# Eight of 64 tiles transposed by VectorE instead of TensorE, with another head and another list of transfers

## The chip, the cores and the metric

The kernel runs on one core of a Trainium2 chip. The metric is the device time of one execution in microseconds, the median of three runs. Five engines work in parallel, each through its own list of instructions in order: TensorE (PE in the profile; its weight loads are PEld), VectorE (DVE), ScalarE (ACT), GpSimd (POOL) and SyncE (SP), which here issues every transfer. Sixteen DMA engines move the data.

## The reference

```python
batch, m, k, n = 16, 512, 1024, 768          # all float32
out = np.matmul(x, weight) + bias + residual
```

So 8192 rows of x, each of 1024 numbers, times a matrix of 1024 x 768, plus a bias row and a residual of the size of the output. In all 33.5 MB of x, 25.2 MB of residual and 3.1 MB of weight are read, and 25.2 MB are written.

## The kernel before

**Tiles.** The 8192 rows are cut into four parts (S = 0 to 3) of 16 tiles (j = 0 to 15) of 128 rows; tile t is 16 S + j. Partition p of a part holds the rows 16 p to 16 p + 15, so that a transfer of several tiles reads one long run a partition. SBUF has room for 16 x tiles (`X`) and 32 rows of residual and output (`R`, one 128 x 768 row of tiles each; W is staged there at first too).

**What is done with a tile.** ScalarE casts the x tile to bf16 (`cast`, L226 by way of `copy`) into one of four buffers `XB`. TensorE transposes it (`transp`, L250): two neighbouring bf16 numbers are taken as one 4-byte word, so that four transposes of 128 x 128 words do the 1024 columns. They go to one of two PSUM buffers `PT`, and VectorE copies them to one of four buffers `XT` (L226). Then TensorE does 8 steps (4 q x 2 e) of one weight load (L268) and two matmuls of 512 and 256 columns (L257) into one of three PSUM buffers `PO` (`mm_all`). VectorE's `finish` adds PSUM to an SBUF row (L229). For the first 14 tiles (`EARLY_END`) it adds the bias and puts the sum in a spare row; GpSimd later adds that to the residual row. For the others GpSimd adds the bias to the residual row beforehand (`pool_adds`), and `finish` waits for that. `ADDS` is the order of GpSimd's first 16 adds.

**The order.** `HEAD_ORDER` is a list written by hand for the first three tiles, which go q by q as the parts of W arrive; `warm` are matmuls on zeros. After it a loop runs over t from 3: cast of tile t + 2, GpSimd's adds, the transposes of tile t + 1, all matmuls of tile t, `finish` of tile t - 1. The last tile's columns are done in two parts.

**The transfers.** `ORDER` is the list of all transfers, in the order in which SP issues them: ('x', S, j0, j1) loads x tiles j0 to j1 - 1 of part S, 'r' residual rows, 'w' a quarter of the weight, 'b' the bias; 's' stores rows, 'c' a part of the last row. `pump` takes from its head whatever may be recorded: an x tile needs the cast of the tile 16 before it, a residual row the store of the row 32 before it, a store its `finish` or add. On the chip SP waits at each entry for what it needs, and all that come after it wait too.

**Waits.** `Program.add` records each operation with the keys it reads and writes, and `Program.emit` turns them into waits. [...]

## Time and profile before

| what | value |
|---|---|
| time, median of 3 runs | 210.14 us (210.11 to 210.18) |
| span of the profiled execution | 208.5 us, 2492 instructions |
| PE busy | 201.6 us (97%) |
| DVE busy | 105.3 us (51%) |
| ACT busy | 66.1 us (32%) |
| POOL busy | 115.2 us (55%) |
| transfers | 87.20 MB, 97.9% of 16 engines' span |
| four transposes of a tile, group of 256 | 38.3 us busy |
| copy of transposed words on VectorE, 64 | 44.1 us, 691 ns each |
| last store | issued at 204.63, landed 2.6 us later |

The three runs' times are those of whole executions; the profiled execution is known by its span, and the runs' median lies 1.6 us above that. Busy shares are means over the span; the rows of the profile name an engine, a line of the kernel, an operation, and the tiles it writes and reads. In an order of time, a row has its start, its length, and in brackets how long the engine had been idle and what ended that. Rows of the busy times by stage have, after each engine's time, the granted TensorE clock, the share of the DMA engines and GB/s.

### The profile page before, as it was taken

What the parts mean: (1) busy time and instruction counts of PE and PEld (TensorE: products, weight loads), DVE (VectorE), ACT (ScalarE), POOL (GpSimd) and SP (SyncE); (2) the same over time, 40 slices, a digit from 0 to 9 for tenths busy, and PEclk for the clock granted to TensorE, in tenths of its full rate; (3) what the DMA queues carried; (4) which work ended last, traced back from release to release, by engine and by line L of the source; (5) the groups of instructions that cost most, each with busy time, mean ns of one, the idle gap of its engine ahead of it and who ended that gap; (6) DMA issues with size and microseconds to landing.
All of it is one profiled execution on the core that took longest, in us unless ns stands there. A gap on an engine that the chain in (4) does not pass through costs nothing.

```text
span 208.5 us, 2492 instructions
## 1 busy us (share of the span) xinstructions
PE 201.6 (97%) x1298; PEld 80.8 (39%) x794; DVE 105.3 (51%) x141; ACT 66.1 (32%) x69; POOL 115.2 (55%) x71
## 2 busy tenths in 40 slices
PE   7899999999999999999999999999999999999991
PEld 2333434443443444344334434433443443344340
DVE  1457555445545543654554454555445545544542
ACT  2444522402640282420280094230092047430000
POOL 1100029859999904999029801999207960899200
PEclk9999999999999999999999999999999999999998
DMA  5999999899999999999998999999999999999985
GB/s 216 425 425 445 426 423 475 385 427 425 485 409 416 449 395 438 453 396 437 410 493 387 432 445 429 443 443 385 423 450 468 416 398 471 415 443 417 427 351 232
DMA packets 4627, 87.20 MB, mean 418 GB/s; under 512 B 516, under 2 KB 644, under 8 KB 1416
## 3 DMA queue, kind: packets, MB, share of 16 engines
q1 hardware_dynamic: 4616, 87.05, 97.9%
q8 instruction: 8, 0.13, 0.2%
q14 instruction: 3, 0.02, 0.0%
HBM read 61.88 MB, written 25.17 MB: 417 GB/s over the span
## 4 chain that ended last, share of the span: by engine, by line
PE 92%; DMA 4%; DVE 1%; SPq 0%; ACT 0%; issue 0%
PE psum_o L257 79%; PE pt L250 13%; DMA x_tile<-in_x_dram 4%; SPq L168 0%; DVE xt L226 0%; ACT xb L226 0%; DVE ro L229 0%; SPq L403 0%; SPq L371 0%
## 5 line engine op out<-in xcount | busy, mean ns | idle before, releaser
L257 PE MATMUL psum_o<-w_sb,xt 128*128 128x256 bf16 (+1 forms) x1024 | 176.6, 326 | 0.5 <-DVE xt L226 0.5
L229 POOL TENSOR_TENSOR ro<-ro,bias_sb 128x768 f32<-128x768 f32 x50 | 88.8, 1817 | 46.9 <-DMA ro<-in_residual_dram 46.9
L226 ACT CAST xb<-x_tile 128x1024 bf16<-128x1024 f32 (+1 forms) x63 | 61.3, 1023 | 117.1 <-DMA x_tile<-in_x_dram 88.6
L268 PEld LDWEIGHTS <-xt 128*128 128x128 bf16 x520 | 50.9, 98 | 102.9 <-issue 101.0
L226 DVE COPY xt<-pt 128x1024 bf16<-128x1024 bf16 x64 | 44.1, 691 | 83.4 <-PE pt L250 83.4
L229 DVE TENSOR_TENSOR ro<-psum_o,ro 128x768 f32<-128x768 f32 (+2 forms) x51 | 47.6, 934 | 6.5 <-POOL ro L229 4.5
L250 PE MATMUL pt<-ident,xb 128*128 128x128 f32 x256 | 38.3, 274 | 0.6 <-DVE xb L226 0.4
L229 POOL TENSOR_TENSOR ro<-ro 128x768 f32<-128x768 f32 x14 | 24.9, 1818 | 25.0 <-DMA ro<-in_residual_dram 24.9
L250 PEld LDWEIGHTS pt<-ident,xb 128*128 128x128 f32 x256 | 29.7, 141 | 15.6 <-issue 12.3
L229 DVE TENSOR_TENSOR ro<-psum_o,bias_sb 128x768 f32<-128x768 f32 x14 | 13.2, 948 | 0.0
L312 PE MATMUL psum_o<-warm 128*128 128x512 bf16 x18 | 6.3, 506 | 1.4 <-DVE warm_a L232 1.4
L226 DVE CAST xb<-x_tile 128x512 bf16<-128x512 f32 (+1 forms) x4 | 1.9, 492 | 6.2 <-DMA x_tile<-in_x_dram 6.2
L226 ACT CAST w_sb<-ro 128x768 bf16<-128x768 f32 x4 | 3.3, 832 | 3.7 <-DMA ro<-in_weight_dram 3.7
L226 POOL CAST w_sb<-ro 128x768 bf16<-128x768 f32 x1 | 0.8, 822 | 6.0 <-DMA ro<-in_weight_dram 6.0
L312 PEld LDWEIGHTS psum_o<-warm 128*128 128x128 bf16 x18 | 2.1, 124 | 4.5 <-issue 2.7
L226 DVE CAST w_sb<-ro 128x768 bf16<-128x768 f32 x3 | 1.7, 557 | 2.0 <-DMA ro<-in_weight_dram 2.0
L226 ACT ACT_TABLE_LOAD x1 | 1.3, 1283 | 0.9 <-SPq L371 0.9
L329 DVE STREAM_SHUFFLE bias_sb<-bias_row 128x768 f32<-128x768 f32 x1 | 1.0, 1007 | 0.0
L232 DVE MEMSET warm<- 128x256 uint32 x1 | 0.3, 272 | 1.1 <-SPq L371 1.1
L232 DVE MEMSET bias_row<- 128x768 f32 x1 | 0.7, 698 | 0.2 <-issue 0.2
L232 POOL MEMSET ident<- 128x128 f32 x1 | 0.2, 204 | 0.5 <-SPq L371 0.5
L320 POOL TENSOR_SCALAR_AFFINE_SELECT ident<-ident 128x128 f32<-128x128 f32 x1 | 0.3, 292 | 0.2 <-POOL ident L232 0.2
(7 smaller groups left out, 0.7 us busy)
## 6 DMA issues: line engine op xcount, KB each, us to landing
out_dram<-ro SPq DMA_DIRECT2D x3, 6144.0 KB, 34.6
x_tile<-in_x_dram SPq DMA_DIRECT2D x3, 5120.0 KB, 24.5
ro<-in_residual_dram SPq DMA_DIRECT2D x3, 3840.0 KB, 32.4
x_tile<-in_x_dram SPq DMA_DIRECT2D x3, 3072.0 KB, 34.0
ro<-in_residual_dram SPq DMA_DIRECT2D x3, 2304.0 KB, 18.7
x_tile<-in_x_dram SPq DMA_DIRECT2D x4, 1024.0 KB, 10.9
x_tile<-in_x_dram SPq DMA_DIRECT2D x2, 2048.0 KB, 23.4
out_dram<-ro SPq DMA_DIRECT2D x1, 3840.0 KB, 13.3
```

Source lines behind the costliest of these rows:

```text
L226: op(eng, lambda e: (e.copy if eng == "act" else e.tensor_copy)(out=dst, in_=src), rd, wr)
L229: op(eng, lambda e: e.tensor_add(out=dst, in0=a, in1=b), rd, wr)
L232: op(eng, lambda e: e.memset(dst, v), [], [wr])
L250: op("pe", lambda e, q=q: e.transpose(out=pt[:, q, :], in_=words[:, ts(q, P)], identity=ident), [("XB", t % XB_N, 2 * q // n_q), "ident"], ...
L257: return e.add_instruction(mybir.InstMatmult(name=nc.get_next_instruction_name(), ins=[e.lower_ap(rhs), e.lower_ap(lhsT, for_matmul_weight ...
L268: op("pe", lambda g: g.ldweights(lhsT), rd)
L312: op("pe", lambda e: e.matmul(PO[i][:, 0:512], lhsT=warm[:, 0:P], rhs=warm, start=True, stop=True), ["warm"], [("PO", i)])
L320: op("pool", lambda e: e.affine_select(out=ident, in_=ident, compare_op=mybir.AluOpType.not_equal, fill=1.0, base=0, pattern=[[-1, P]], ch ...
L329: op("dve", lambda e: e.stream_shuffle(out=bias_sb, in_=bias_row, mask=[0] * QUAD), ["bias_row"], ["bias"])
```

## The change

Four pairs of tiles, (21, 22), (45, 46), (52, 53) and (60, 61), are no longer transposed on TensorE. Each pair is cast by ScalarE into a buffer of its own (`XB2`), six tiles before its first tile instead of two. VectorE then transposes it (`blocks`) from SBUF to SBUF (`XT2`): the 128 x 128 words of a block are cut into 4 x 4 squares of 32 x 32, and one instruction takes the squares (a, b) of all four q and both tiles from partitions 32 a to 32 a + 31, transposes each, and writes them to partitions 32 b to 32 b + 31. That is 16 instructions of 32 partitions x 256 words a pair, in place of two copies of 128 x 1024 bf16. `turn` places two of them behind `finish` and two behind the next copy, in each of the four turns of the loop from d - 5 to d - 2, where d is the pair's first tile.

In every turn of the loop the transposes of tile t + 1 now stand between the two halves of the matmuls of tile t, and `finish` of tile t - 1 before them on VectorE.

In the head, tile 3 is loaded behind W, cast and transposed at the end, and three warming matmuls go. GpSimd's first 16 adds are in the order of the tiles. The list of transfers has other cuts: x tiles 10 to 15 of part 0 in one, behind eight residual rows instead of six; the x parts cut at 9, 7 and 8 instead of 6; the store of part 1 cut at 11.

```diff
+DT = [21, 45, 52, 60]
+DT_LEAD = 6
-ADDS = [10, 14, 3, 2, 4, 15, 11, 1, 5, 13, 7, 6, 12, 9, 0, 8]
+ADDS = [0, 1, 2, 3, 4, 5, 6, 7, 8, 9, 10, 11, 12, 13, 14, 15]
 HEAD_ORDER = [('cast', 0, 'v'), ('cast', 1, 's'), ('tr', 0), ('tr', 1), ('wc', 0, 0, 's'), ('wc', 0, 1, 'g'),
- ('warm', 3), ('mm', 0, 0), ('mm', 1, 0), ('cast', 2, 'sv'), ('cast', 3, 'sv'), ('warm', 3),
- ('tr', 2), ('tr', 3), ('wc', 1, 0, 's'), ('wc', 1, 1, 'v'), ('mm', 2, 0), ('mm', 0, 1),
- ('mm', 1, 1), ('mm', 2, 1), ('wc', 2, 0, 's'), ('wc', 2, 1, 'v'), ('mm', 0, 2), ('mm', 1, 2),
- ('mm', 2, 2), ('wc', 3, 0, 's'), ('wc', 3, 1, 'v'), ('bias',), ('cast', 4, 'sv'), ('mm', 0, 3),
- ('fin', 0), ('mm', 1, 3), ('mm', 2, 3)]
-ORDER = [('x', 0, 0, 2), ('w', 0, 0, 2), ('x', 0, 2, 4), ('w', 1, 0, 2), ('b', 0, 0, 0), ('w', 2, 0, 2),
- ('w', 3, 0, 2), ('x', 0, 4, 6), ('x', 0, 6, 10), ('r', 0, 0, 6), ('x', 0, 10, 14),
- ('r', 0, 6, 16), ('x', 0, 14, 16), ('x', 1, 0, 6), ('r', 1, 0, 6), ('x', 1, 6, 16),
- ('r', 1, 6, 16), ('s', 0, 0, 16), ('x', 2, 0, 6), ('r', 2, 0, 6), ('x', 2, 6, 16),
- ('r', 2, 6, 16), ('s', 1, 0, 16), ('x', 3, 0, 6), ('r', 3, 0, 7), ('x', 3, 6, 16),
- ('r', 3, 7, 16), ('s', 2, 0, 16), ('s', 3, 0, 10), ('s', 3, 10, 13),
- ('s', 3, 13, 15), ('c', 3, 15, 0), ('c', 3, 15, 1)]
+ ('warm', 3), ('mm', 0, 0), ('mm', 1, 0), ('cast', 2, 'sv'), ('tr', 2), ('mm', 2, 0), ('wc', 1, 0, 's'),
+ ('wc', 1, 1, 'v'), ('mm', 0, 1), ('mm', 1, 1), ('mm', 2, 1), ('bias',), ('wc', 2, 0, 's'),
+ ('wc', 2, 1, 'v'), ('mm', 0, 2), ('mm', 1, 2), ('mm', 2, 2), ('wc', 3, 0, 's'), ('wc', 3, 1, 'v'),
+ ('cast', 3, 'sv'), ('mm', 0, 3), ('fin', 0), ('mm', 1, 3), ('tr', 3), ('mm', 2, 3), ('cast', 4, 's')]
+ORDER = [('x', 0, 0, 2), ('w', 0, 0, 2), ('x', 0, 2, 3), ('w', 1, 0, 2), ('b', 0, 0, 0), ('w', 2, 0, 2),
+ ('w', 3, 0, 2), ('x', 0, 3, 4), ('x', 0, 4, 6), ('x', 0, 6, 10), ('r', 0, 0, 8), ('x', 0, 10, 16),
+ ('r', 0, 8, 16), ('x', 1, 0, 9), ('r', 1, 0, 6), ('x', 1, 9, 16), ('r', 1, 6, 16), ('s', 0, 0, 16),
+ ('x', 2, 0, 7), ('r', 2, 0, 8), ('x', 2, 7, 16), ('r', 2, 8, 16), ('s', 1, 0, 11), ('x', 3, 0, 8),
+ ('r', 3, 0, 8), ('s', 1, 11, 16), ('x', 3, 8, 16), ('r', 3, 8, 16), ('s', 2, 0, 16), ('s', 3, 0, 10),
+ ('s', 3, 10, 13), ('s', 3, 13, 15), ('c', 3, 15, 0), ('c', 3, 15, 1)]
...
     def transp(t):
-        if t < n_t:
+        if t < n_t and t not in two:
...
+    two = {t + i: i for t in DT for i in range(2)}
+
+    def blocks(t, n0, n1):
+
+        src = XB2.bitcast(FP32).rearrange("p i (q c) -> p i q c", c=P)
+        dst = XT2.rearrange("p i q m e -> p i q (m e)").bitcast(FP32)
+        for n in range(n0, n1):
+            a, b = divmod(n, P // QUAD)
+            op("dve", lambda e, a=a, b=b: e.transpose(
+                out=dst[ts(b, QUAD), :, :, ts(a, QUAD)], in_=src[ts(a, QUAD), :, :, ts(b, QUAD)]),
+               [("XB2", 0), ("XB2", 1)], [("XT2", n)])
...
+    per = (P // QUAD) ** 2
+
+    def turn(h):
+        for d in DT:
+            i, n = h - 2 * (d - DT_LEAD + 1), 2 * (DT_LEAD - 2)
+            if 0 <= i < n:
+                blocks(d, per * i // n, per * (i + 1) // n)
+
     for t in range(HEAD, n_t):
-        cast(t + 2)
+        for d in DT:
+            if t == d - DT_LEAD:
+                cast(d)
+                cast(d + 1)
+        if t + 2 not in two:
+            cast(t + 2)
         pool_adds(t + 1)
-        transp(t + 1)
         if t < n_t - 1:
-            mm_all(t, range(n_q))
+            mm_all(t, range(n_q // 2))
         finish(t - 1)
         pool_adds(t + 1)
+        turn(2 * t)
+        transp(t + 1)
+        turn(2 * t + 1)
+        if t < n_t - 1:
+            mm_all(t, range(n_q // 2, n_q))
```

More of the change, by code (lines that the diff above doesn't have):

```diff
@@ L151 @@
     XT = fixed(sb, "xt", XT_N, [P, n_q, P, 2], BF16)
+    (XB2,) = fixed(sb, "xb_two", 1, [P, 2, K], BF16)
+    (XT2,) = fixed(sb, "xt_two", 1, [P, 2, n_q, P, 2], BF16)
     PO = fixed(ps, "psum_o", HEAD, [P, N], FP32)
@@ L238, in cast @@
             rd, wr = [("X", t % XR)], [("XB", t % XB_N, i) for i in range(2)]
+            if t in two:
+                dst, wr = XB2[:, two[t], :], [("XB2", two[t])]
             if how == "sv":
@@ L267, in mm @@
         lhsT, rd = XT[t % XT_N][:, q, :, e], [("XT", t % XT_N)]
+        if t in two:
+            lhsT, rd = XT2[:, two[t], q, :, e], [("XT2", n) for n in range((P // QUAD) ** 2)]
         op("pe", lambda g: g.ldweights(lhsT), rd)
```

## The prediction

> **What bounds the kernel now.** I read the page from the top: busy shares, slices, transfer queues, the chain that ended last.

> ```profile
> PE 201.6 (97%) x1298; PEld 80.8 (39%) x794; DVE 105.3 (51%) x141; ACT 66.1 (32%) x69; POOL 115.2 (55%) x71
> ...
> DMA  5999999899999999999998999999999999999985
> ...
> q1 hardware_dynamic: 4616, 87.05, 97.9%
> ...
> PE 92%; DMA 4%; DVE 1%; SPq 0%; ACT 0%; issue 0%
> ```

> Two resources are full at once. TensorE (PE) is busy 97% and carries 92% of the chain. But the transfer engines are busy 97.9% of the same span, and a faster TensorE takes no byte away. So I asked next where the transfer engines have any room, with the busy times by stage:

> ```profile
> 3.00:190.00 187.00, 185.85 (x1206) 74.41 (x731) 96.17 (x128) 64.66 (x67) 110.37 (x63) 1.00 1.01 431
> 190.00:200.00 10.00, 10.00 (x68) 3.88 (x39) 5.56 (x8) 0.00 (x0) 4.09 (x3) 1.00 0.96 412
> 200.00:204.00 4.00, 4.00 (x26) 1.93 (x20) 2.18 (x3) 0.00 (x0) 0.00 (x0) 1.00 0.77 325
> 204.00:206.00 2.00, 0.14 (x2) 0.00 (x0) 0.42 (x1) 0.00 (x0) 0.00 (x0) 1.00 0.98 391
> ```

> The last but one number is the DMA share: 1.01 from 3 to 190 us, 0.96 for ten microseconds, 0.77 for four. The mean engine waits for results for 0.4 + 0.9 us in the tail. The slowest engine does not wait at all. The landing records of the last five stores end at 201.69, 204.44, 206.28, 206.93 and 207.27 us. These steps of 2.75, 1.84, 0.65 and 0.34 us are what eight packets of 347, 232, 84 and 45 ns take. The next slowest engine lands the last store 0.3 us earlier, the fastest 0.5. So there are two ends side by side: compute earlier by any amount brings almost nothing, and compute later by more than about 0.4 us (between 0.3 and 0.5) shows in full.

> The steady state of one tile, in order of time:

> ```profile
> 25.25 0.60 PE L250 MATMUL pt<-ident,xb 128*128 128x128 f32 x4
> ...
> 25.68 2.76 PE L257 MATMUL psum_o<-w_sb,xt 128*128 128x512 bf16 x16
> 25.89 0.69 DVE L226 COPY xt<-pt 128x1024 bf16<-128x1024 bf16 x1 [1.48 <-PE pt L250]
> ...
> 26.50 0.95 DVE L229 TENSOR_TENSOR ro<-psum_o,bias_sb 128x768 f32<-128x768 f32 x1
> ...
> 28.29 0.60 PE L250 MATMUL pt<-ident,xb 128*128 128x128 f32 x4
> ```

> A tile takes 28.29 - 25.25 = 3.035 us (as exact over many tiles); its matmuls take 28.29 - 25.68 = 2.60, its four transposes the other 0.435. VectorE (DVE) does one copy and one add, 1.64 us, and then waits 1.48 us.

> **The change part by part.** The profiled span is 208.5 us and the median of the runs 210.14, so 1.6 us lie around the span; I add differences to the median.

> *Removed from TensorE:* 4 transposes of 8 tiles, 8 x 0.435 = 3.48 us, all on PE's path.

> *Added to VectorE:* 16 strips a pair, 64 in all, each 32 partitions x 256 words; 8 copies of 0.691 go. The trace has no strip. Its nearest rows:

> ```profile
> L229 DVE TENSOR_TENSOR ro<-psum_o,ro 128x768 f32<-128x768 f32 x49 | 46.5, 949 | 5.6 <-POOL ro L229 4.5 <-PE psum_o L257 1.1
> ...
> L329 DVE STREAM_SHUFFLE bias_sb<-bias_row 128x768 f32<-128x768 f32 x1 | 1.0, 1007 | 0.0
> ...
> L232 DVE MEMSET warm<- 128x256 uint32 x1 | 0.3, 272 | 1.1 <-SPq L371 1.1
> ...
> L229 DVE TENSOR_TENSOR ro<-psum_o,ro 128x256 f32<-128x256 f32 x1 | 0.4, 425 | 0.2 <-PE psum_o L257 0.2
> ```

> The low bound is the memset of 256 words, 272 ns. The add of 256 words takes 425. The two adds give (949 - 425)/512 = 1.02 ns an element; the shuffle, the nearest in kind, less 512 elements is 1007 - 524 = 483 ns, the high bound. I take 440 ns, just above the add of the same size. On average that is harmless: 64 x 0.44 - 8 x 0.69 = 22.6 us more, 128 of 208 us busy. But the strips are not spread: `turn` puts four into each of four tile periods before a pair, between the add and the copy that the next tile's matmuls wait for. In such a period VectorE has 0.949 + 0.691 + 4 x 0.44 = 3.40 us to do, and TensorE 3.035.

> Does it overlap? Two full-width adds in a row take 1.82 us (at 18.61), 0.08 less than twice 0.949. With 0.08 off at six hand-overs the load is 2.92 us, under 3.035. No pair in the trace goes from one group of partitions to another, as each strip does; I give no credit for an overlap that only full-width pairs show, and keep 2.92 as the other end. [...]

> At 3.40 VectorE slips 0.365 a period. In the first period of a window the copy ends about 0.15 + 0.95 + 0.88 + 0.69 = 2.67 us after the matmuls' start, 0.3 before it is needed (0.06 for the hand-over). So the next copies are late by 0.07, 0.365 and 0.365: 0.8 us of PE wait a pair, 3.2 for four, against 0.87 saved a pair.

> *The head.* x tile 3 (0.52 MB, 1.2 us at the rate below) now lies behind W, so W's last three parts land 1.2 us earlier and tile 3 starts at about 18.4 instead of 19.6. One round of three warming matmuls goes too; it stood in a wait. This gain is spent at once, by

> *the list of transfers.* Tiles 10 to 13 came by themselves; now 10 to 15 come in one, behind eight residual rows instead of six. ScalarE and GpSimd show when transfers landed:

> ```profile
> 34.93 3.89 ACT L226 CAST xb<-x_tile 128x1024 bf16<-128x1024 f32 x4 [7.81 <-DMA x_tile<-in_x_dram]
> 46.47 1.99 ACT L226 CAST xb<-x_tile 128x1024 bf16<-128x1024 f32 x2 [7.66 <-DMA x_tile<-in_x_dram]
> ```

> Between them 10 residual rows and 2 x tiles, 4.98 MB, took 11.54 us: 0.432 MB/us. Two rows and two tiles more are 1.84 MB, 4.25 us, so tile 10 lands at 39.2 and its cast (1.04) ends at 40.2. Its transposes stand in the middle of tile 9, due at 18.4 + 6 x 3.035 + 1.3 = 37.9. TensorE waits 2.4 us, and tile 10 starts at 40.3 + 0.435 + 1.3 = 42.05, where it stood at 22.65 + 6 x 3.035 = 40.86: 1.2 us later, head included. The later x parts land before their casts by 2 us or more, but for tile 16, where I find ScalarE level with TensorE: the casts of 21 and 22 (1.94 us) now precede that of 17. SP's queue stays fed: the one new wait on it, that of the last residual part for the split-off store of part 1 to land, begins with 8 x tiles (4.19 MB, 9.7 us) still queued.

> *The order of the adds.* GpSimd gets residual rows at 31.85 (30.03 before, two rows more), does 8 at 1.78, waits for 46.5, does six, and finishes add 14 at 58.9, 15 at 60.7. VectorE's add of tile 14 is ready at 57.2 and waits 1.7 us there; the copy of 16 behind it ends at 60.5 where 60.2 was due: 0.3. Row 16 lands at 62.9 (46.47 plus 7.08 MB at the rate above), so GpSimd's add of it ends at 64.7; VectorE, behind add 15, one add, four strips and a copy, is there at 64.2. That costs the first window another 0.5.

> *The transposes in the middle of a tile* cost nothing outside the windows: the copy ends 2.7 us after the tile's start, due at 3.04. That cover of 0.3 is what the strips use up.

> Sum on TensorE: 1.2 + 0.3 + 0.5 + 3.2 - 3.48 = 1.7 us later at the end. Less the 0.4 that the slowest transfer engine hides: 1.3 us, **211.4**.

> **The rivals.**

> *Strips overlap, or cost under 0.41 us in a row (load up to 3.30).* Then TensorE ends up to 2 us earlier (1.2 + 0.3 - 3.48) and the slowest transfer engine sets the end as now. Nothing shrinks its work: the same bytes, one transfer more (eight packets an engine; under 0.1 us by the fixed time that 309 ns for a packet of 8 KB and 611 for one of 16 KB leave). 210.1, between 209.8 and 210.5. For it: DMA share 1.01. Against it: the add of 256 words already takes 0.425.

> *A gap at every hand-over.* The cast that ends at 6.45 releases TensorE at 6.50: a waited-for hand-over takes 0.05. With 0.06 at six hand-overs the load is 3.76, 0.725 a period, 2.1 us a pair: 1.2 + 0.3 + 0.5 + 8.4 - 3.48 = 6.9 later on TensorE, 216.6. At the high bound of 483 ns without gaps the load is 3.57 and a pair costs 1.4: 4.1 later, 213.8; at 425 ns it is 3.34 and 0.58, and the time 210.6.

> *The tail shrinks.* If the engines' spread (2.3 us at the tenth row of the last store) comes out smaller, earlier results let go of the 1.3 us that the mean engine waits: up to 209.1. It decides only if VectorE keeps up and the slowest engine loses its lag of 1.3 us; I see nothing that makes it.

> **How the numbers follow.** About 0.2%, 0.42 us, can be told from no change. Strips without overlap at 425 to 483 ns, 210.6 to 213.8: 0.38. Overlap, end set by transfers: 0.40, of which 0.32 within 0.2%, 0.04 on either side. Gaps as well, 213.8 to 218: 0.15. The tail shrinks: 0.07, all faster. Faster 0.11, same 0.33 (0.01 of it from the first case's edge), slower 0.56. The range from 209.8 to 216.3 leaves out most of the shrunken tail and the upper part of the gaps; the forecast case's own range is 210.6 to 213.8.

> **What would show it.** Right: strips of about 440 ns starting no earlier than the one before ends; TensorE's weight loads waiting for VectorE's copies, 0.3 to 0.4 us at three tiles before each pair, and some 2 us for the cast of tile 10; VectorE busy near 128 us; transfer share over the span a little lower. Wrong: strips in a row at under 0.41 us, no such waits, TensorE done by 203 and the last store landing at 207 as before. The forecast also falls if the wait at tile 10 is absent, or if a transfer starves.

## The result, and the profile after

The changed kernel takes 213.34 us (median of 4 runs, 213.27 to 214.57), the kernel before 210.12 (4 runs, 209.97 to 210.18). The ratio is 1.0164, interval 1.0145 to 1.0184: slower by 3.2 us, where the forecast was slower by 1.3. The span of the profiled execution went from 208.5 to 211.5 us. Two of the kernels below (the spread strips and fewer bytes) each had one execution of over 740 us; without it their medians would be lower by at most 0.07 us.

The page of the kernel after, the lines that answer to those of before:

```profile
PE 198.5 (94%) x1239; PEld 77.1 (36%) x759; DVE 132.4 (63%) x196; ACT 66.8 (32%) x69; POOL 115.3 (55%) x71
...
q1 hardware_dynamic: 4760, 87.05, 96.5%
...
PE 44%; DMA 22%; DVE 21%; POOL 6%; issue 3%; SPq 2%; DVEq 0%; POOLq 0%
...
L267 DVE STREAM_TRANSPOSE xt_two<-xb_two 32x256 f32<-32x256 f32 x64 | 27.9, 435 | 1.1
```

TensorE is busy 3.1 us less, close to the 3.48 that were saved on it, and ends later: it waits more. The chain of work that ended last shows on whom. It was 92% TensorE; now half of it goes through residual transfers, VectorE and GpSimd. A strip takes 435 ns.

The busy times by stage of the kernel after. The columns are the stretch, its length, then PE, PEld, DVE, ACT and POOL, the granted clock, the share of the transfer engines and GB/s. The share counts each transfer packet whole in the stretch in which it starts, so in short stretches it can be above 1, or 0 while older packets still run:

```profile
3.00:190.00 187.00, 179.76 (x1131) 69.73 (x687) 119.91 (x177) 64.33 (x66) 112.39 (x64) 1.00 1.01 430
190.00:200.00 10.00, 9.59 (x59) 3.25 (x34) 7.09 (x11) 1.05 (x1) 2.17 (x2) 1.00 0.84 359
200.00:204.00 4.00, 4.00 (x29) 1.73 (x18) 1.98 (x3) 0.00 (x0) 0.00 (x0) 1.00 0.87 367
204.00:206.00 2.00, 2.00 (x12) 0.88 (x9) 1.31 (x2) 0.00 (x0) 0.00 (x0) 1.00 0.29 110
```

Up to 190 us the transfer engines are as full as before. Then their share falls to 0.84 (0.96 before), and between 204 and 206 us they have almost nothing to do (0.29) while TensorE is fully busy; before, TensorE was done by then. Compute now sets the end alone. TensorE ends at 207.52 (204.14 before, +3.38), the last store lands at 210.23 (207.27 before, +2.96). The 0.42 between the two differences is the part that the slowest transfer engine used to hide.

VectorE in the second half of one window, the kernel after, in order of time:

```profile
141.43 0.96 DVE L231 TENSOR_TENSOR ro<-psum_o,ro 128x768 f32<-128x768 f32 x1
142.41 0.88 DVE L267 STREAM_TRANSPOSE xt_two<-xb_two 32x256 f32<-32x256 f32 x2
143.30 0.69 DVE L228 COPY xt<-pt 128x1024 bf16<-128x1024 bf16 x1
144.02 0.89 DVE L267 STREAM_TRANSPOSE xt_two<-xb_two 32x256 f32<-32x256 f32 x2
144.92 0.96 DVE L231 TENSOR_TENSOR ro<-psum_o,ro 128x768 f32<-128x768 f32 x1
```

No row has a bracket: VectorE waits for nobody, and one round takes 144.92 - 141.43 = 3.49 us, where TensorE's tile takes 3.035. TensorE waits for the rest. The waits of its weight loads in the kernel after (total us, times, longest):

```profile
PEld L286 <- DVE xt L228: 12.0, 20, 1.0
```

### The profile page after: what moved, and what is told of

Its sections match the earlier page's. It is cut to its first block, busy times and chain, and to the rows that moved or that the text cites. A ratio compares the mean times of both kernels' runs of the same rounds, so it can differ in the third digit from the quotient of the medians.

```text
span 211.5 us, 2498 instructions
## 1 busy us (share of the span) xinstructions
PE 198.5 (94%) x1239; PEld 77.1 (36%) x759; DVE 132.4 (63%) x196; ACT 66.8 (32%) x69; POOL 115.3 (55%) x71
## 3 DMA queue, kind: packets, MB, share of 16 engines
q1 hardware_dynamic: 4760, 87.05, 96.5%
## 4 chain that ended last, share of the span: by engine, by line
PE 44%; DMA 22%; DVE 21%; POOL 6%; issue 3%; SPq 2%; DVEq 0%; POOLq 0%
PE psum_o L273 39%; DMA ro<-in_residual_dram 22%; DVE xt_two L267 9%; DVE ro L231 7%; POOL ro L231 6%; DVE xt L228 5%; PE pt L254 5%; SPq L170 2%; SPq L438 0%; DVEq L104 0%; POOLq L104 0%; SPq L406 0%
## 5 line engine op out<-in xcount | busy, mean ns | idle before, releaser
L273 PE MATMUL psum_o<-w_sb,xt 128*128 128x256 bf16 (+1 forms) x875 | 154.4, 325 | 5.1 <-DVE xt L228 3.6
L228 ACT CAST xb<-x_tile 128x1024 bf16<-128x1024 f32 (+1 forms) x55 | 54.7, 1028 | 113.1 <-PE pt L254 67.5
L286 PEld LDWEIGHTS <-xt 128*128 128x128 bf16 x456 | 44.6, 98 | 96.6 <-issue 81.5
L228 DVE COPY xt<-pt 128x1024 bf16<-128x1024 bf16 x56 | 38.6, 691 | 30.8 <-PE pt L254 30.5
L254 PE MATMUL pt<-ident,xb 128*128 128x128 f32 x224 | 33.6, 273 | 2.3 <-ACT xb L228 2.3
L254 PEld LDWEIGHTS pt<-ident,xb 128*128 128x128 f32 x224 | 26.0, 140 | 15.7 <-issue 11.3
L267 DVE STREAM_TRANSPOSE xt_two<-xb_two 32x256 f32<-32x256 f32 x64 | 27.9, 435 | 1.1
L273 PE MATMUL psum_o<-w_sb,xt_two 128*128 128x256 bf16 (+1 forms) x125 | 21.9, 325 | 0.2
L286 PEld LDWEIGHTS <-xt_two 128*128 128x128 bf16 x64 | 6.3, 98 | 13.6 <-issue 13.6
L228 ACT CAST xb_two<-x_tile 128x1024 bf16<-128x1024 f32 x8 | 8.0, 1043 | 7.9 <-DMA x_tile<-in_x_dram 7.9
```

The costliest lines, as they stand in the source:

```text
L228: op(eng, lambda e: (e.copy if eng == "act" else e.tensor_copy)(out=dst, in_=src), rd, wr)
L254: op("pe", lambda e, q=q: e.transpose(out=pt[:, q, :], in_=words[:, ts(q, P)], identity=ident), [("XB", t % XB_N, 2 * q // n_q), "ident"], ...
L267: op("dve", lambda e, a=a, b=b: e.transpose(out=dst[ts(b, QUAD), :, :, ts(a, QUAD)], in_=src[ts(a, QUAD), :, :, ts(b, QUAD)]), [("XB2", 0) ...
L273: return e.add_instruction(mybir.InstMatmult(name=nc.get_next_instruction_name(), ins=[e.lower_ap(rhs), e.lower_ap(lhsT, for_matmul_weight ...
L286: op("pe", lambda g: g.ldweights(lhsT), rd)
```

## The experiments

All edits are to the kernel after.

**No pairs.** Everything else of the change stays.

```diff
-DT = [21, 45, 52, 60]
+DT = []
```

> The changed kernel with no pair on VectorE (DT empty): all 64 tiles transposed by TensorE, the new head, list, order of adds and place of the transposes kept. Theory (two causes: overloaded windows on VectorE, and a late start of tiles 10 to 16): in the changed kernel's trace the four windows stretch 12 tile periods by 5.1 us over 3.04 each, 0.36 of which the two short tiles behind them give back, so 4.7 us go, and 3.48 us of transposes come back: 213.3 - 1.3 = 212.1 us. Rival A (the strips are the whole loss): about 210.1 us, as before. Rival B (the head, the list and the adds are the whole loss, the windows hide behind it): 213.3 us.

Measured: 212.06 us (6 runs, two of them 2 us longer than the others), ratio to the kernel before 1.0079 [1.0062, 1.0096]. The pairs with their strips cost 213.34 - 212.06 = 1.28 us net, although they take 3.48 us off TensorE. The other 1.9 us belong to the rest of the change.

**The strips spread.** The same 16 strips a pair over six tile periods instead of four, at most three in one; two pairs moved by one tile, so that a window, which now begins a tile earlier, does not begin before the tiles of the pair ahead of it are multiplied. It ran twice.

```diff
-DT = [21, 45, 52, 60]
+DT = [21, 45, 53, 61]
...
-    per = (P // QUAD) ** 2
+    SLOTS = [0, 1, 1, 2, 1, 2, 1, 2, 1, 2, 3, 0]
...
-            i, n = h - 2 * (d - DT_LEAD + 1), 2 * (DT_LEAD - 2)
-            if 0 <= i < n:
-                blocks(d, per * i // n, per * (i + 1) // n)
+            i = h - 2 * (d - DT_LEAD)
+            if 0 <= i < len(SLOTS):
+                blocks(d, sum(SLOTS[:i]), sum(SLOTS[:i + 1]))
```

> The changed kernel with the strips of a pair spread thinner: 1 at the end of the loop's turn d - 6, 3 in each of d - 5 to d - 2, 3 in d - 1, where no copy is made; so that a period holds 0.957 + 0.70 + 3 x 0.445 = 2.99 us on VectorE instead of 3.49 against 3.04 on TensorE. Pairs at 21, 45, 53, 61, so that a pair's strips do not start before the one before it is used. Theory (load over the period makes the wait): no wait of 0.45 us at three tiles before each pair, at most 0.3 at the pair's first tile; TensorE done 3 to 4 us earlier than 207.5, and the time at the transfer engines' end, 210.1 to 210.4 us. Rival A (strips cost by their number, wherever they stand): 213.3. Rival B (the late start is the loss): 212.5 to 213.3 us.

> The changed kernel with strips spread 1, 3, 3, 3, 3, 3 and pairs 21, 45, 53, 61, once more, for its profile: 210.9 us as measured before. Theory: no waits of 0.45 us before the pairs 45, 53 and 61; the waits at tiles 10 and 16 as in the changed kernel; TensorE done near 204 us and the last store landed at 207.3 to 208.

Measured: 210.94 us the first time, ratio 1.0041 [1.0023, 1.0059], and 211.02 the second, 1.0048 [1.0028, 1.0067]. Spreading alone takes back 2.3 to 2.4 of the 3.2 us. The pairs that cost 1.28 now gain 212.06 - 210.98 = 1.1. The ten runs of the second time lie in two groups, five at 210.3 to 210.6 and five at 211.5 to 211.9; the second group has a lower mean granted clock (0.987 to 0.990 against 0.995 to 1.000). What may lie behind that is in the last section. In the first group, to which the profiled execution belongs, spreading takes back 2.9 of the 3.2 us: TensorE ends at 204.50 instead of 207.52, no tile before the pairs 45, 53 and 61 starts late any more, and the waits at tiles 10 (2.2 us) and 16 are about as in the kernel after.

**The old list of transfers and the old order of GpSimd's adds, in part 0 and 1.** The first pair goes, because its window would need x tiles that this list brings later. The pairs' windows are those of the change.

```diff
-DT = [21, 45, 52, 60]
+DT = [45, 52, 60]
...
-ADDS = [0, 1, 2, 3, 4, 5, 6, 7, 8, 9, 10, 11, 12, 13, 14, 15]
+ADDS = [10, 14, 3, 2, 4, 15, 11, 1, 5, 13, 7, 6, 12, 9, 0, 8]
...
- ('w', 3, 0, 2), ('x', 0, 3, 4), ('x', 0, 4, 6), ('x', 0, 6, 10), ('r', 0, 0, 8), ('x', 0, 10, 16),
- ('r', 0, 8, 16), ('x', 1, 0, 9), ('r', 1, 0, 6), ('x', 1, 9, 16), ('r', 1, 6, 16), ('s', 0, 0, 16),
+ ('w', 3, 0, 2), ('x', 0, 3, 4), ('x', 0, 4, 6), ('x', 0, 6, 10), ('r', 0, 0, 6), ('x', 0, 10, 14),
+ ('r', 0, 6, 16), ('x', 0, 14, 16), ('x', 1, 0, 6), ('r', 1, 0, 6), ('x', 1, 6, 16), ('r', 1, 6, 16), ('s', 0, 0, 16),
```

> The changed kernel with the old list of transfers for parts 0 and 1 from x tile 6 on and the old order of adds; the pair (21, 22), which that list can't serve in time, is left to TensorE; the other three pairs and their four strips a period stay. Theory: the wait of 2.3 us at tile 10 and that of 0.4 us at tile 16 go, with them the first window (1.68 us of waits, 0.87 saved): 213.3 - 3.5 = 209.8, so the transfer engines' end, 210.1 us; up to 211.4 us if the add of row 16, done at 63.8 us in the kernel before, now holds back the copy of tile 18 that stands behind it on VectorE. Rival A (strips are the whole loss): three quarters of 3.2 us stay, 212.5 us. Rival B (list and head are the loss): 210.1 us.

Measured: 212.07 us, ratio 1.0087 [1.0071, 1.0102]: a miss by 2 us. VectorE of this kernel, in order of time, shows why:

```profile
63.77 0.96 DVE L231 TENSOR_TENSOR ro<-psum_o,ro 128x768 f32<-128x768 f32 x1 [2.98 <-POOL ro L231]
64.64 0.68 DVE L228 COPY xt<-pt 128x1024 bf16<-128x1024 bf16 x1
```

The add waits 2.98 us for GpSimd, and the copy, whose input is long ready, waits behind it. TensorE's next matmuls then wait 0.98 us for that copy. The same place in the kernel before:

```profile
62.33 0.69 DVE L226 COPY xt<-pt 128x1024 bf16<-128x1024 bf16 x1 [1.48 <-PE pt L250]
63.80 0.96 DVE L229 TENSOR_TENSOR ro<-psum_o,ro 128x768 f32<-128x768 f32 x1 [0.78 <-POOL ro L229]
65.36 0.69 DVE L226 COPY xt<-pt 128x1024 bf16<-128x1024 bf16 x1 [0.61 <-PE pt L250]
```

The add waits here too, and ends at 64.76, but the copy stood ahead of it. The next copy still finds VectorE idle for 0.61 us, so nothing reaches TensorE. This is a part of the change that the forecast had not priced: `finish` now stands ahead of the copy.

**Both repairs.** The old list and order of adds with the spread strips, on the pairs 45, 53 and 61; `ORDER`, `ADDS` and `SLOTS` as in the two diffs above.

```diff
-DT = [21, 45, 52, 60]
+DT = [45, 53, 61]
```

> Both: the old list of parts 0 and 1 and the old order of adds, pairs 45, 53, 61, strips spread 1, 3, 3, 3, 3, 3. TensorE should be done by 203.5 us, earlier than the 204.1 of the kernel before. Theory (the slowest transfer engine sets the end): 210.1 us, within 0.3, whatever TensorE saves. Rival C (TensorE sets the end): below 209.5 us. Rival D (strips or the new place of the transposes cost something not yet seen): above 210.6 us.

Measured: 210.48 us, ratio 1.0014 [1.0004, 1.0024], with TensorE done at 203.97. VectorE of this kernel in a spread window:

```profile
136.57 0.96 DVE L231 TENSOR_TENSOR ro<-psum_o,ro 128x768 f32<-128x768 f32 x1
137.55 0.43 DVE L267 STREAM_TRANSPOSE xt_two<-xb_two 32x256 f32<-32x256 f32 x1
137.99 0.69 DVE L228 COPY xt<-pt 128x1024 bf16<-128x1024 bf16 x1
138.71 0.88 DVE L267 STREAM_TRANSPOSE xt_two<-xb_two 32x256 f32<-32x256 f32 x2
139.61 0.96 DVE L231 TENSOR_TENSOR ro<-psum_o,ro 128x768 f32<-128x768 f32 x1
```

With three strips the round is 139.61 - 136.57 = 3.04 us, TensorE's own period: VectorE is full and, in the spread windows, holds nobody up. The fourth strip is what the windows of the change do not fit.

**No pairs, with the old list and the old order of adds.** `ORDER` and `ADDS` as in the diff of the old list.

```diff
-DT = [21, 45, 52, 60]
+DT = []
```

> No pair on VectorE, the old list of transfers for parts 0 and 1 and the old order of adds; what stays of the change is the new head and the new place of finish and the transposes in a tile's period. Theory (finish, which waits for GpSimd's add of a row that has just landed, now stands ahead of the copy that TensorE waits for): in the run with the old list TensorE lost 1.2, 0.7 and 0.6 us at tiles 18, 24 and 34 this way, 2.5 in all; less 0.5 us gained in the head and 0.4 hidden by the transfer engines: 210.1 + 1.6 = 211.7 us. Rival (what is left of the change costs nothing): 210.1 us.

Measured: 211.40 us, ratio 1.0064 [1.0049, 1.0079]. Against 212.06 without pairs, list and order of adds are worth 0.66.

**The copy ahead of `finish` again**, in the kernel above.

```diff
-        finish(t - 1)
-        pool_adds(t + 1)
         turn(2 * t)
         transp(t + 1)
+        finish(t - 1)
+        pool_adds(t + 1)
         turn(2 * t + 1)
```

> The kernel before this one in the list with a single swap: the transposes and their copy are recorded ahead of finish of tile t - 1, still in the middle of the period. Theory: the waits at tiles 18, 24 and 34 go, TensorE ends some 0.5 us before the 204.1 of the unchanged kernel, and the transfer engines set the end: 210.1 us. Rival (the middle of the period is itself the loss, since the copy has 1.3 us less room): 211.7 us as without the swap.

Measured: 210.41 us, ratio 1.0020 [1.0010, 1.0030]. Moving two lines is worth 0.99 us. VectorE of this kernel, where the wait for GpSimd is as long as in the kernel before and again falls behind the copy:

```profile
62.98 0.69 DVE L228 COPY xt<-pt 128x1024 bf16<-128x1024 bf16 x1 [1.48 <-PE pt L254]
64.43 0.96 DVE L231 TENSOR_TENSOR ro<-psum_o,ro 128x768 f32<-128x768 f32 x1 [0.77 <-POOL ro L231]
```

**The copy first, and nothing else**: the diff just shown, in the kernel after, with its windows, list and order of adds.

> The changed kernel with that swap alone: pairs, list and adds as changed. Theory: the wait of 0.45 us at tile 16 and the 0.5 us that the first window loses to GpSimd's adds go; the wait at tile 10 (2.3) and the overload in the windows (0.455 a period) stay: 213.3 - 0.9 = 212.4 us, and at least 212. Rival A (strips are the whole loss): 213.3. Rival E (the order on VectorE is the whole loss): 210.1 us.

Measured: 214.77 us, ratio 1.0227 [1.0212, 1.0242], slower by 1.4 than the kernel after: a miss. TensorE does end some 0.6 us earlier. But in a full window the strips and the copy now come before the add, and the add that the store of the last ten tiles waits for starts at 192.84 instead of 190.84. The store is issued at 193.82 (191.83 after), and the busy times by stage of this kernel show that the transfer engines began nothing until then:

```profile
191.00:194.00 3.00, 2.71 (x18) 0.79 (x9) 2.90 (x6) 1.05 (x1) 1.78 (x2) 1.00 0.00 0
```

A DMA share of 0.00 says that no packet starts in these three microseconds. By the start and length of every packet, the mean transfer engine stands idle for 3.6 us between 189 and 195, against 1.7 in the kernel after. So the transfers have work to the very end again, and what TensorE gained is lost: fifteen of the sixteen engines land the last store by 210.08, where the kernel after is done at 210.23. The sixteenth engine lands it at 211.80, 1.7 us behind the others, which is more than the whole slowdown. An instruction fetch of 16 KB, 0.96 us long, starts at 204.52 among the last stores and can be a part of that lag; the trace does not say on which engine it ran, and the rest stays open. In these kernels, then, the copy first gains where VectorE has room (0.99 us without pairs) and nothing in full windows.

**All repairs.** The kernel of both repairs with the copy first as well.

```diff
-        finish(t - 1)
-        pool_adds(t + 1)
         turn(2 * t)
         transp(t + 1)
+        finish(t - 1)
+        pool_adds(t + 1)
         turn(2 * t + 1)
```

> Old list and old adds, pairs 45, 53 and 61 with strips spread 1, 3, 3, 3, 3, 3, and the copy ahead of finish. TensorE should be done near 201.5 to 202 us, 2 to 2.5 us before the unchanged kernel. Theory (the slowest transfer engine sets the end): 210.1 us, within 0.2, last store landed at 207.0 to 207.3 as before. Rival C (TensorE sets the end): 208 us or less.

Measured: 210.50 us, ratio 1.0023 [1.0010, 1.0036]. TensorE's last result is stored from 202.52, against 204.63 in the kernel before, 2.1 us earlier, and the last store lands at 207.41, against 207.27. Compute was made faster, as the change set out to do, and nothing came of it. The time is even 0.4 us above the 210.1 that the theory named, as it is with both repairs; that rest is open. The stages of this kernel:

```profile
200.00:204.00 4.00, 2.03 (x14) 1.09 (x12) 1.70 (x3) 0.00 (x0) 0.00 (x0) 1.00 0.93 387
204.00:206.00 2.00, 0.00 (x0) 0.00 (x0) 0.00 (x0) 0.00 (x0) 0.00 (x0) 0.93 0.82 329
```

TensorE is idle from 202 us, while the transfer engines work at 0.93 and 0.82.

**Fewer bytes.** The kernel above without loading the last four residual rows of part 3 (1.57 MB, 3.6 us at the measured 0.432 MB/us); these four tiles are added to what lies in SBUF. It ran twice.

```diff
+                nl = nj - 4 if (S, j0) == (3, 8) else nj
-                dma(R[:, t0 % RR:t0 % RR + nj, :], res_d[S, :, j0:j1, :], [], rows(t0, t0 + nj))
+                dma(R[:, t0 % RR:t0 % RR + nl, :], res_d[S, :, j0:j0 + nl, :], [], rows(t0, t0 + nl))
```

> The kernel with everything mended (old list and adds, spread strips, copy first; 210.5 us, TensorE done at 202), with the last four residual rows left unloaded: their adds take what lies in those rows. 1.57 MB less, 3.6 us of the transfer engines; all engines' work stays. Theory (the transfer engines' bytes set the end of that kernel): 3.6 us less on the slowest engine, until the end is set by the last add, 202.5 plus 2.3 us to land: 207.5 to 208.2 us. Rival (the last results set the end): 210.5 us, no change.

> The kernel with fewer bytes once more, for where its time goes: it came out at 209.14 us where 207.5 to 208.2 was expected. If the transfer engines still set the end, TensorE is done near 202.0 and the last store lands 2 us or more after the last result is handed over, with the engines' share near 1.0 to the end. If TensorE sets it, TensorE is done near 204 and the last store lands within about 3 us of it. The time should be 209.1 again.

Measured: 209.14 us, ratio 0.9956 [0.9939, 0.9972], then 209.33, ratio 0.9962 [0.9943, 0.9982]. Fewer bytes and the same compute are faster by 1.2 to 1.4, so the transfers do set the end there; TensorE is done at 202.0 in both kernels. Only a third of the 3.6 us came, and the repeat shows where most of the rest is:

```profile
186.00:188.30 2.30, 2.30 (x17) 0.93 (x10) 2.21 (x5) 1.05 (x1) 2.30 (x2) 1.00 0.35 150
```

The transfer engines finish their earlier work one after the other, from 186.98 to 189.72 us, and the store of the last ten tiles is issued at 188.27, the moment VectorE's add of the tenth ends (188.24). By the start and length of every packet, the mean engine stands idle for 1.35 us between 186 and 189.6. With all bytes no engine stands idle in this stretch (its share is 1.09 from 186 to 188.3). About 1 us is left, and the landing records say where it lies, not why: fourteen engines land the last store by 204.90, one at 205.32 and the last at 206.24. So neither picture of the repeat's expectation holds in full: TensorE is done at 202.0, but the share is only 0.27 from 204 to 206 us.

**Do strips overlap at all?** Each strip of the kernel after cut into two halves of 32 x 128 words, which lie on the same partitions one after the other. One run.

```diff
-            op("dve", lambda e, a=a, b=b: e.transpose(
-                out=dst[ts(b, QUAD), :, :, ts(a, QUAD)], in_=src[ts(a, QUAD), :, :, ts(b, QUAD)]),
-               [("XB2", 0), ("XB2", 1)], [("XT2", n)])
+            for i in range(2):
+                op("dve", lambda e, a=a, b=b, i=i: e.transpose(
+                    out=dst[ts(b, QUAD), i, :, ts(a, QUAD)], in_=src[ts(a, QUAD), i, :, ts(b, QUAD)]),
+                   [("XB2", 0), ("XB2", 1)], [("XT2", n)])
```

> The changed kernel with each strip cut into two of 128 words, one for each tile of the pair: two in a row now read and write the same partitions, while every second hand-over still changes them. It measures the hand-over by itself; the time will be longer, 217 to 221 us, as a period holds eight halves. From the strip of 435 ns for 256 words and 1.02 ns a word, a half takes about 305 ns. Theory (a hand-over between different partitions gives no overlap): within a pair of halves the second starts about 80 ns before the first ends, as two full-width adds do; from pair to pair it starts 0 to 20 ns after the end. Rival (a transposing instruction never overlaps): no overlap within a pair either.

Measured: 224.37 us, slower than expected. The group of halves of this kernel, and VectorE in order of time:

```profile
66.31 1.28 DVE L268 STREAM_TRANSPOSE xt_two<-xb_two 32x128 f32<-32x128 f32 x4
67.61 0.69 DVE L228 COPY xt<-pt 128x1024 bf16<-128x1024 bf16 x1
...
L268 DVE STREAM_TRANSPOSE xt_two<-xb_two 32x128 f32<-32x128 f32 x128 | 38.7, 302 | 3.3
```

A half takes 302 ns, where half a strip would be 218: 435 = 302 + 128 x 1.04 ns, so some 170 ns of each strip would not depend on its size, an estimate from these two sizes. Four halves take 1.28 us, not the 1.21 of four times 302: the second half starts 34 ns after the first has ended, the next pair, on other partitions, 13 ns after. No strip overlaps the one before it, on the same partitions or not. So the rival holds here, not the theory. Behind an add it is otherwise. In the kernel after:

```profile
60.98 0.96 DVE L231 TENSOR_TENSOR ro<-psum_o,ro 128x768 f32<-128x768 f32 x1 [0.29 <-POOL ro L231]
61.86 0.87 DVE L267 STREAM_TRANSPOSE xt_two<-xb_two 32x256 f32<-32x256 f32 x2
```

The first of these strips starts at the same partitions as the add and 84 ns before the add has ended; a strip on other partitions starts 14 ns after an add (at 142.41, for one).

## Why the prediction was right or wrong

The direction and the mechanism were right; the size was not. Set against the forecast's sum, with the starts of tiles (their first weight load) in the two traces (us on TensorE):

| step of the sum | forecast | measured |
|---|---|---|
| tile 10 late, head included | +1.2 | +1.70 |
| copy of 16 behind `finish` | +0.3 | +0.40 |
| row 16, in the first window | +0.5 | +0.55 |
| four windows | +3.2 | +4.21 |
| transposes saved | -3.48 | -3.48 |
| TensorE's end | +1.7 | +3.38 |
| hidden by the slowest transfer engine | -0.4 | -0.42 |

**The strip and what stands about it.** 440 ns were forecast and 435 measured, without overlap between strips. x tiles 10 to 15 were to land at 39.2 and their first cast starts at 39.24; TensorE was to wait 2.4 us and waits 2.30; residual row 16 was to land at 62.9 and GpSimd's add of it starts at 63.04:

```profile
39.24 5.87 ACT L228 CAST xb<-x_tile 128x1024 bf16<-128x1024 f32 x6 [11.99 <-DMA x_tile<-in_x_dram]
40.34 0.66 PE L254 MATMUL pt<-ident,xb 128*128 128x128 f32 x4 [2.30 <-ACT xb L228]
59.14 0.96 DVE L231 TENSOR_TENSOR ro<-psum_o,ro 128x768 f32<-128x768 f32 x1 [2.23 <-POOL ro L231]
67.50 1.47 PE L273 MATMUL psum_o<-w_sb,xt 128*128 128x512 bf16 x8 [0.51 <-DVE xt L228]
```

These are lines of the order of time of the kernel after: arrival, wait, and the two places where GpSimd's order reaches TensorE by way of VectorE's copy.

**The step that failed first: the windows.** The load of a round was put at 3.40 us, without gaps, and was 3.49. Its instructions take 3.39 of it (the strips a little less than forecast, the add 0.957 instead of 0.949); the other 0.10 are gaps at the six hand-overs to or from a strip: 31 ns after the copy, about 14 at the others. The slip is 0.455 a round, not 0.365. And the forecast counted 0.07 in the first full round and two more slips, where the second, third and fourth windows lose 0.22 to 0.25, then 0.45, then 0.46 to 0.48 in their rounds, 1.14 to 1.16 each in all. The first loses 0.55 more, to row 16. Together 5.14, of which 0.38 come back in the two short tiles behind each window: 4.76 with row 16, against 3.7. The gaps were a rival's term (0.06 at six hand-overs, 216.6). It was kept apart from the likeliest case as if a gap were all or nothing; the small one that was there lay between the two.

**The second: tile 10.** The new start of tile 10 was forecast at 42.05 and is 42.03, and the old one, forecast at 40.86, is 40.76. Both were right within 0.1 and their difference was not the lag. In the kernel before, a tile's start comes after the transposes of the next tile; in the changed one these come in the middle. At the end of the tile the changed kernel is 42.03 + 3.035 - 40.76 - 2.60 = 1.70 late. The two starts of tile 3, 19.39 and 18.34, compare in the same false way: the head gained 1.05 - 0.435, about 0.6, where the forecast took 1.2.

**The third: "the transposes in the middle of a tile cost nothing outside the windows".** The cover of 0.3 us holds only while `finish` does not wait. Ahead of the copy, `finish` hands GpSimd's lateness to TensorE. With the new list and adds this was in the sum in part (0.3 and 0.5); with the old list it cost 0.99 us by itself, which the forecast had no term for. It is no part of the miss in the table, whose terms close; it is a wrong step that another list would have made dear.

**The rivals.** Strips that overlap fall with 435 ns, the rounds of 3.49 us and the halves. The engines' spread did come out smaller, 0.2 us at the tenth row of the last store (202.18 to 202.38) where it was 2.3, but only because all of them had waited for VectorE's add; with TensorE as the end, that gained nothing. The 1.3 us of waiting that this rival built on were too many: read from the shares by stage they are 0.4 + 0.9, by the start and length of every packet 0 + 0.56. VectorE is busy 132.4 us where about 128 were named, and its copies hold up TensorE by 0.45 us in a full round where 0.3 to 0.4 were.

**The end.** The 0.4 us that the transfers hide were right. The two fulls that the forecast put side by side were shown: with all repairs TensorE is done 2.1 us earlier and the time stays at 210.5.

Going back from after to before by medians: spread strips give back 2.3 to 2.4. By another path, without the pairs 1.28, with the old list and adds 0.66, with the copy first 0.99, which leaves 210.41 against 210.07. These steps are not independent: the copy first brings 0.99 there, and with the full windows that kernel is slower by 1.4. The last 0.3 us is partly the landing (207.39 against 207.27); the rest is open, as are 0.2 of the 3.2 us that lie around the span (1.84 us after, 1.6 before). No kernel here that does the whole work beats the one before.

## What to carry to other kernels

When work moves from a full engine to one with idle time, add up the receiving engine's work in the stretch where it lands, gaps included, and compare that with the other's period; a mean share of 63% hid rounds of 3.49 us against 3.04. Put the instruction that the full engine waits for ahead of one that itself may wait for a third engine, as long as the engine that runs both has room. And before speeding up one engine, ask what ends next to it: here the slowest transfer engine had work to the end, TensorE was only 0.4 us from setting the end itself, and no saving on TensorE could show.

## What the runs showed of the hardware

```profile
40.59 0.66 PE L254 MATMUL pt<-ident,xb 128*128 128x128 f32 x4 [2.42 <-ACT xb L228]
...
42.00:43.00 1.00, 1.00 (x5) 0.28 (x2) 0.00 (x0) 1.00 (x2) 1.00 (x2) 0.50 0.92 393
43.00:45.00 2.00, 2.00 (x8) 0.44 (x3) 0.96 (x1) 1.32 (x2) 2.00 (x2) 0.50 1.16 498
```

It stays there for 3.41 us, from 41.90 to 45.32, and sixteen matmuls, as many as a tile has (the row that starts at 41.08), take 4.44 us, where those of the kernel after (at 40.83) take 2.76. Two of that kernel's six runs are 2 us longer (213.9) than the other four (about 212). In the kernel after the clock stayed at 1.00 in the profiled execution until TensorE was done, one run of four is 1.2 us longer. With the spread strips half of the ten runs are, with a mean clock of 0.99; for these I infer the same event from the mean clock alone.

What decides it is not shown; three traces give a hint. In the profiled executions of the kernels before and after, the stretch at full clock lasts 201.39 and 204.80 us. The difference is 3.41 us, as long as the half clock lasts without pairs, and the stretches are 59 and 60 steps of 3.413 us. Without pairs, in the step before the fall, 38.49 to 41.90, TensorE is idle for 2.10 us in all. In the kernel after, with steps counted from the start of the full clock at 5.87, the wait lies across two, and the one with more of it (36.59 to 40.00) has 2.01 us of idle time: no fall. At the ends of the kernels before and after, the clock falls at 206.69 and 210.67, and the steps ahead of that have 2.55 and 3.14 us of idle time. So a wait of this length may halve the clock or not by where it lies between two steps. That is the author's estimate from these three traces; no run varied it by itself.

**Instruction fetches among the packets.** In the kernel before, one of 16 KB starts about every 24 us (at 23.84, 47.38 and 71.48, for instance; eight in all) and takes 1.0 to 1.1 us on a transfer engine. With the copy first and nothing else, one of 0.96 us lies among the last stores, and one engine lands the last store 1.7 us behind the other fifteen.
